# Two pairs of heads per chain step, and the output product in three groups and one, in a mixer on one core

## Chip, cores and metric

One core of one Trainium2 chip. The metric is the device time in microseconds of one execution of the whole program; of several executions the median counts.

## The reference, cut to what matters

The program computes one layer of two networks after each other on a sequence of 512 tokens of 1024 features. The change lies in the first part of the first layer, `hybrid_mixer`: a bidirectional RWKV-7 scan over 8 heads of 64, and a pooling branch, whose joined outputs are multiplied by `w_out`.

```python
def wkv7_scan(r, w, k, v, kk, a, reverse):
    def step(state, inp):
        r_t, w_t, k_t, v_t, kk_t, a_t = inp
        sa = jnp.einsum('bhvk,bhk->bhv', state, -kk_t)
        state = (state * w_t[:, :, None, :]
                 + sa[..., :, None] * (kk_t * a_t)[..., None, :]
                 + v_t[..., :, None] * k_t[..., None, :])
        return state, jnp.einsum('bhvk,bhk->bhv', state, r_t)

def hybrid_mixer(h, ...):
    ...
    for d in range(N_DIR):
        ...
        o = o + wkv7_scan(rh, heads(decay), kd, vh, kk, heads(a), reverse=(d == 1))
    ...
    return jnp.concatenate([y_rwkv, y_pool], axis=-1) @ w_out

x = x + hybrid_mixer(rmsnorm(x, norm1_w[l]), ...)
```

## The kernel before

The scan is computed in chunks of 64 tokens: 8 chunks, both directions d at once, and the heads in four pairs, 0 to 3, whose two heads e lie on the two halves of the 128 partitions. For a pair there are five pieces of work:

- *terms* (`wkv_terms`): elementwise products of the projections. They give AR (the receiving side) and BK (the sending side) of all chunks. For pairs 2 and 3 both go to memory (`spill`) and are loaded again by `wkv_load`.
- *scores* (`wkv_scores`): 64x64 products of BK with AR in each chunk (L672) and transposes of BK (L679). BK is kept with zeros beside each head's half, so that one product over all 128 partitions takes one head.
- *inverse* (`wkv_inverse`): a triangular inverse T of each chunk's 64x64 block. The diagonal blocks are solved on VectorE (L712 to L733), after a trip of the scores through memory that lays them out anew (X); T comes back through memory, and two levels of products on TensorE follow (L750, L755, L757), with copies between them. L760 is the last add of a level.
- *chain* (`wkv_chain`): the recurrence over the 8 chunks, one step after the other. A step multiplies the state Z with the scores (L801), copies to ysb on ScalarE (L803), multiplies with T (L816), copies to Z on VectorE (L820), multiplies with BN (L825) and adds the decayed state (L775, with sw from POOL, L811) to get the next state. L808 and L830 gather the output in the PSUM tile o, which L838 and L839 add into oT at the end. Each head of a pair has a PSUM tile pm of its own. The part of Z that holds the values comes from memory (vnat, L783).
- *wkv_out*: group norm, bonus and gate, with two products over 512 columns (L855, L860).

Pairs 0 and 1 have their scores and inverses beside the projections. After the projections a loop over j runs the chains of the pairs one after the other; the scores and inverse of pairs 2 and 3 are placed before or after the chains of pairs 0 and 1 by small lists (POST, INVP), and a scheduler orders each engine's instructions by their priorities (PRI, set by `hp_`). The result y of pairs 0 to 2 is written to memory and loaded again.

The output product has eight terms: a term is 128 rows of `w_out` with one y (terms 0 to 3 are the pairs of heads, 4 to 7 the pooling groups). It runs in split single precision, three products of 512 columns each for one block of 128 tokens (L129 to L131 in `mm3`; the helper `split`, L136 and L137, makes the two parts of an operand). Eight PSUM tiles `acc` hold all blocks and both halves of the columns; seven terms are added beside chain 3, the term of pair 3 last, and then eight adds (L510) bring in x.

At the start of the mixer POOL writes the zeros of BK, C and M (L242). The zeros' loop runs twice over w.C and w.M, which are two names for one tile each.

Of the kernel before, what the change touches and what calls it, by code (L numbers as in the profile page):

```python
# [9 lines left out]
F32 = mybir.dt.float32  # L10
F32R = mybir.dt.float32r
# [213 lines left out]
def mixer(g, I):  # L225
# [3 lines left out]
    with es:  # L229
        w = Ctx()  # L230
        kp = es.enter_context(tc.tile_pool(name="m_keep", bufs=1))
        w.p = es.enter_context(tc.tile_pool(name="w_p", bufs=2))
        w.a = es.enter_context(tc.tile_pool(name="w_a", bufs=2))
# [12 lines left out]
        w.pr = es.enter_context(tc.tile_pool(name="w_pr", bufs=1, space=PSUM))  # L246


        mid = es.enter_context(ExitStack())
        with ExitStack() as tmp, tc.tile_pool(name="m_h", bufs=1, side="right") as hp, tc.tile_pool(name="m_w", bufs=WINB, side="right") as wp, \  # L250
# [31 lines left out]
            w.i = mid.enter_context(tc.tile_pool(name="w_i", bufs=1, reuse_waits="tile"))  # L282
# [138 lines left out]
        rt = dict(side="right", reuse_waits="tile")  # L421
        tmp = es.enter_context(ExitStack())
        p2 = tmp.enter_context(tc.tile_pool(name="w_p2", bufs=1, reuse_waits="tile"))
        res = es.enter_context(ExitStack())
        w.z = res.enter_context(tc.tile_pool(name="w_z", bufs=3, **rt))
        aR = res.enter_context(tc.tile_pool(name="w_ar", bufs=2, **rt))
        w.y = res.enter_context(tc.tile_pool(name="w_y", bufs=2, **rt))
        w.g = res.enter_context(tc.tile_pool(name="w_g", bufs=1, **rt))
        w.pc = es.enter_context(tc.tile_pool(name="w_pc", bufs=1, space=PSUM, reuse_waits="tile"))
        for j in range(4):  # L430
            if j == 3:
                tmp.close()
# [12 lines left out]
                ys = {}
            if j < 2 and POST[j] == 0:
                with hp_(tc, PRI[20 + j]):
                    Ps.append(wkv_load(g, w, j + 2, w.p if j else p2, aR))
                with hp_(tc, PRI[10 + j]):
                    wkv_scores(g, w, Ps[j + 2])  # L450
            if j < 2 and INVP[j] == 0:
                if POST[j]:
                    with hp_(tc, PRI[20 + j]):
                        Ps.append(wkv_load(g, w, j + 2, w.p if j else p2, aR))
                    with hp_(tc, PRI[10 + j]):
                        wkv_scores(g, w, Ps[j + 2])
                with hp_(tc, PRI[8 + j]):
                    wkv_inverse(g, w, Ps[j + 2])
# [1399 lines left out]
```

## Time and profile before

| | |
|---|---|
| device time, median of 3 runs | 3271.31 us (3246.06 to 3279.7) |
| the profiled execution's own time | 3270.52 us |
| its span, first to last instruction | 3268.7 us |
| mean granted clock of TensorE | 0.947 |
| mixer | from 0 to 598 us |
| busy in the span: PE, DVE, ACT, POOL | 94%, 65%, 40%, 44% |

In the profile PE is TensorE's products, PEld its weight loads, DVE VectorE, ACT ScalarE, POOL GpSimd and SP the engine that issues most DMAs. Line numbers are those of the kernel before. A matrix product in single precision shows as two rows, and rows of products overlap, so their starts and not their durations tell how fast they go. The granted clock is the share of TensorE's full clock (2.4 GHz) that it was given; 0.50 is 1.2 GHz.

### The profile page before, as it was taken

The page shows a single profiled execution, that of the slowest core. Times are in us where ns is not written, and L with a number is a line of the kernel's source. Part 1 is how long each engine was busy: PE and PEld are TensorE (multiplying, and loading weights), DVE is VectorE, ACT ScalarE, POOL GpSimd, SP SyncE. Part 2 cuts the span into 40 slices and gives each one's busy share as a digit, 9 for nine tenths or more (in the row PEclk, how much of TensorE's full clock was granted, in tenths as well). Part 3 has the DMA queues.
Part 4 walks back from the last instruction along what each step waited for, and adds up shares of the span by engine and source line. Part 5 has one row for each costly group of instructions (what it writes and reads, how often), then busy time and mean ns, then how long its engine had stood idle before and what let it go on. Part 6 is the DMA issues. An engine that isn't in the chain of part 4 may idle for free.

```text
span 3268.7 us, 45544 instructions
## 1 busy us (share of the span) xinstructions
PE 3079.9 (94%) x16467; PEld 2632.9 (81%) x16467; DVE 2139.5 (65%) x3955; ACT 1298.5 (40%) x2244; POOL 1442.2 (44%) x1234
## 2 busy tenths in 40 slices
PE   7688999798889999999999999999999989999999
PEld 6467887687889999998998778778888878778887
DVE  5876434578997887888887876565664143456631
ACT  4333212333665333333333435564443255244431
POOL 4533222434766766667776555343222242222221
PEclk9788857899999999999999999999999999899999
DMA  5354313412447888888887874113232212132312
GB/s 171 92 121 130 81 37 112 143 46 91 155 178 267 311 302 317 303 311 306 313 313 279 285 242 145 57 48 104 97 98 90 90 62 70 39 106 94 101 61 100
DMA packets 282877, 512.30 MB, mean 157 GB/s; under 512 B 78054, under 2 KB 166902, under 8 KB 280860
## 3 DMA queue, kind: packets, MB, share of 16 engines
q1 hardware_dynamic: 244636, 373.05, 34.6%
q0 software_dynamic: 36864, 134.23, 11.5%
q8 instruction: 131, 2.15, 0.3%
q10 hardware_dynamic: 1152, 2.10, 0.2%
q14 instruction: 94, 0.77, 0.1%
HBM read 461.28 MB, written 49.99 MB: 156 GB/s over the span
## 4 chain that ended last, share of the span: by engine, by line
PE 68%; DVE 14%; DMA 6%; issue 5%; POOL 4%; ACT 2%; SPq 0%; POOLq 0%; DVEq 0%; ACTq 0%
PE pu L130 5%; PE pu L129 5%; PE pu L131 5%; DVE R L1093 4%; PE S L129 3%; PE S L131 3%; PE S L130 3%; PE o L129 3%; PE o L130 3%; PE o L131 3%; PE dn L129 2%; PE dn L130 2%; PE dn L131 2%; PE pj L129 2%; PE pj L130 2%
## 5 line engine op out<-in xcount | busy, mean ns | idle before, releaser
L129 PE MATMUL S<-hTh,uh 128*128 128x384 f32 x1024 | 362.2, 354 | 0.6 <-ACT gl L984 0.6
L131 PE MATMUL S<-hTh,ul 128*128 128x384 f32 x1024 | 347.2, 339 | 7.0 <-POOL ul L137 4.6
L130 PE MATMUL S<-hTl,uh 128*128 128x384 f32 x1024 | 346.8, 339 | 0.0
L1158 POOL TENSOR_TENSOR vl<-raw,vh 128x1024 fp32r<-128x1024 f32 (+1 forms) x128 | 282.0, 2203 | 94.3 <-ACT vh L1156 92.5
L130 PE MATMUL o<-vl,ah 128*128 128x512 f32 x768 | 299.5, 391 | 5.6 <-DVE vl L1160 5.0
L131 PE MATMUL o<-vh,al 128*128 128x512 f32 x768 | 298.2, 389 | 0.0
L129 PE MATMUL pu<-hTh,wuh 128*128 128x512 f32 (+2 forms) x736 | 282.7, 384 | 3.7 <-ACT wuh L136 3.7
L130 PE MATMUL pu<-hTl,wuh 128*128 128x512 f32 (+2 forms) x736 | 282.1, 383 | 0.0
L129 PE MATMUL o<-vh,ah 128*128 128x512 f32 x768 | 279.3, 393 | 2.4 <-ACT vh L1156 2.4
L131 PE MATMUL pu<-hTh,wul 128*128 128x512 f32 (+2 forms) x736 | 281.2, 383 | 0.0
L1132 DVE SCALAR_TENSOR_TENSOR out<-r,coef,out 128x1024 f32<-128x1024 f32 x127 | 215.9, 1700 | 64.5 <-DMA r<-in_v_r,code 63.9
L137 POOL TENSOR_TENSOR wul<-raw,wuh 128x1024 fp32r<-128x1024 f32 x44 | 106.5, 2420 | 336.8 <-ACT wuh L136 336.8
L1126 DVE SCALAR_TENSOR_TENSOR junk<-r,h 128x1024 bf16<-128x1024 f32 x128 | 203.7, 1592 | 68.5 <-DMA r<-in_u_r,code 67.8
L136 ACT ACTIVATE uh<-raw 128x1024 fp32r<-128x1024 f32 x136 | 144.3, 1061 | 252.6 <-PE S L130 210.0
L1123 POOL DMA_INDIRECT r<-in_u_r,code x128 | 164.8, 1287 | 114.5 <-DVE junk L1126 105.4
L1123 POOL DMA_INDIRECT r<-in_v_r,code x128 | 172.3, 1346 | 79.6 <-DVE out L1132 58.8
L129 PEld LDWEIGHTS S<-hTh,uh 128*128 128x128 f32 x1024 | 195.0, 190 | 9.8 <-issue 1.7
L131 PEld LDWEIGHTS S<-hTh,ul 128*128 128x128 f32 x1024 | 194.4, 190 | 8.7 <-POOL ul L137 5.2
L130 PEld LDWEIGHTS S<-hTl,uh 128*128 128x128 f32 x1024 | 195.0, 190 | 4.6
L137 POOL TENSOR_TENSOR wl<-raw,wh 128x384 fp32r<-128x384 f32 (+3 forms) x90 | 95.8, 1067 | 203.6 <-ACT wh L136 186.8
L130 PEld LDWEIGHTS o<-vl,ah 128*128 128x128 f32 x768 | 144.2, 188 | 36.6 <-DVE vl L1160 9.6
L136 ACT ACTIVATE ah<-a 128x384 fp32r<-128x384 f32 x128 | 67.0, 524 | 265.5 <-PE o L130 259.8
(513 smaller groups left out, 8136.2 us busy)
## 6 DMA issues: line engine op xcount, KB each, us to landing
raw<-in_u_l SPq DMA_DIRECT2D x128, 512.0 KB, 5.7
raw<-in_v_r SPq DMA_DIRECT2D x128, 512.0 KB, 5.3
raw<-in_w_up SPq DMA_DIRECT2D x88, 512.0 KB, 3.4
wscr<-st SPq DMA_DIRECT2D x12, 2048.0 KB, 6.9
W<-wscr SPq DMA_DIRECT2D x32, 768.0 KB, 7.6
raw<-in_w_dn SPq DMA_DIRECT2D x88, 256.0 KB, 2.5
wir<-in_w_in_l SPq DMA_DIRECT2D x38, 256.0 KB, 2.8
raw<-in_w_d_l SPq DMA_DIRECT2D x48, 192.0 KB, 2.4
```

Of the source, the lines that this page charges most:

```text
L129: nc.tensor.matmul(out=out, lhsT=l[0], rhs=r[0], start=start, stop=False)
L130: nc.tensor.matmul(out=out, lhsT=l[0], rhs=r[1], start=False, stop=False)
L131: nc.tensor.matmul(out=out, lhsT=l[1], rhs=r[0], start=False, stop=stop)
L136: nc.scalar.activation(out=hi, in_=src, func=AF.Copy)
L137: (eng or nc.vector).tensor_tensor(out=lo, in0=src, in1=hi.bitcast(F32), op=ALU.subtract)
L1093: (G if u == 1 and t0 % 16 == 0 else V).tensor_scalar(out=R[:, u], in0=iota, scalar1=i2s[:, t:t + 1], scalar2=gateT[:, t:t + 1], op0=ALU.i ...
L1123: G.indirect_dma_start(out=r, out_offset=None, in_=I["u_r" if n < 128 else "v_r"], in_offset=bass.IndirectOffsetOnAxis(ap=code3[:, s:s + 1 ...
L1126: V.scalar_tensor_tensor(out=junk, in0=r, scalar=1.0, in1=h3, op0=ALU.mult, op1=ALU.mult, accum_out=dots[:, s:s + 1])
L1132: V.scalar_tensor_tensor(out=out3, in0=r, scalar=coef[:, s:s + 1], in1=(g.x[:, 3] if s == 0 else out3), op0=ALU.mult, op1=ALU.add)
L1158: G.tensor_tensor(out=vl[:, 0:at_], in0=vraw[:, 0:at_], in1=vh[:, 0:at_].bitcast(F32), op=ALU.subtract)
```

## The change

BK loses its zero halves: it is kept as [128, 8, 2, 64], and the score products take 64 partitions each, with the two heads' products in turn. The scores and inverses of pairs 2 and 3 are emitted right behind the projections, ahead of all chains, without priorities and lists. `wkv_chains` takes two pairs and does each part of a step for both (pairs 0 and 1 first, then 2 and 3); a pair has one PSUM tile pm for both heads, and one copy to ysb. After the first two chains their pools are closed, and in that memory lie new tiles for Z, the output weights and xa, a copy of x that is loaded by one DMA of 2 MB. The output product is summed in groups of two terms, (4, 5), (6, 7), (0, 1): each group goes through a PSUM tile of six products into xa by an add on VectorE, beside chains 2 and 3. The last group (2, 3) goes into x after them. y isn't written to memory any more. `wkv_out` gets its PSUM from another pool, and its tile t shares memory with vt.

```diff
-        w.BK = [kp.tile([128, 8, 2, 2, 64], F32, name=f"BK{d}") for d in range(2)]
+        w.BK = [kp.tile([128, 8, 2, 64], F32, name=f"BK{d}") for d in range(2)]
+        w.oT = [kp.tile([128, S], F32, name=f"oT{j}") for j in range(4)]
         w.C = [kp.tile([128, 8, 128], F32, name="C")] * 2
         w.M = [kp.tile([128, 8, 128], F32, name="M")] * 2
-        for d in range(2):
-            for t in (w.BK[d].rearrange("p c e a t -> p c (e a t)"), w.C[d], w.M[d]):
-                n = t.shape[2] // 2
-                for e in range(2):
-                    G.memset(t[64 * e:64 * e + 64, :, n * (1 - e):n * (2 - e)], 0.0)
+        for t in (w.C[0], w.M[0]):
+            for e in range(2):
+                G.memset(t[64 * e:64 * e + 64, :, 64 * (1 - e):64 * (2 - e)], 0.0)
...
-        for j in range(4):
-            if j == 3:
-                tmp.close()
-                mid.close()
-                op = es.enter_context(tc.tile_pool(name="m_o", bufs=3, reuse_waits="tile"))
-                acc = {}
...
-            if j < 2 and INVP[j] == 0:
-                if POST[j]:
-                    with hp_(tc, PRI[20 + j]):
-                        Ps.append(wkv_load(g, w, j + 2, w.p if j else p2, aR))
-                    with hp_(tc, PRI[10 + j]):
-                        wkv_scores(g, w, Ps[j + 2])
-                with hp_(tc, PRI[8 + j]):
-                    wkv_inverse(g, w, Ps[j + 2])
-            with hp_(tc, PRI[j]):
-                wkv_chain(g, w, Ps[j])
...
+        pB = res.enter_context(tc.tile_pool(name="w_pb", bufs=2, side="right", **rt))
+        w.pc = es.enter_context(tc.tile_pool(name="w_pc", bufs=1, space=PSUM, **rt))
+
+        def chain_pools(st):
+            w.z = st.enter_context(tc.tile_pool(name="w_z", bufs=2, **rt))
+            w.y = st.enter_context(tc.tile_pool(name="w_y", bufs=2, **rt))
+
+        chain_pools(early)
+        for j in (2, 3):
+            Ps.append(wkv_load(g, w, j, pB, pB))
+            wkv_scores(g, w, Ps[j])
+            wkv_inverse(g, w, Ps[j])
+        wkv_chains(g, w, Ps[0:2])
+        early.close()
+        chain_pools(es)
+        op = es.enter_context(tc.tile_pool(name="m_o", bufs=3, **rt))
+        w.g = es.enter_context(tc.tile_pool(name="w_g", bufs=1, **rt))
+        xa = es.enter_context(tc.tile_pool(name="w_x", bufs=1, **rt)).tile([128, NT, D], F32, name="xa")
+        nc.sync.dma_start(out=xa, in_=I["x"].rearrange("(c p) d -> p c d", p=128))
...
+            def part(half, tb):
+                t, hs = slice(tb * 128, (tb + 1) * 128), slice(half * 512, (half + 1) * 512)
+                p = w.pi.tile([128, S], F32, tag="i", name="acc")
+                for n in range(len(ks)):
+                    mm3(nc, p, (ys[n][0][:, t], ys[n][1][:, t]), wos[half, n], n == 0, n == len(ks) - 1)
+                V.tensor_tensor(out=dst[:, tb, hs], in0=p, in1=xa[:, tb, hs], op=ALU.add)
...
+        wkv_chains(g, w, Ps[2:4])
+        ys = [wkv_out(g, w, Ps[j]) for j in range(2)]
+        out_terms((4, 5), None, xa)
+        out_terms((6, 7), None, xa)
+        out_terms((0, 1), ys, xa)
...
+        ys = [wkv_out(g, w, Ps[j]) for j in (2, 3)]
...
+        out_terms((2, 3), ys, g.x, True)
...
-            for e in range(2):
-                p = w.ps.tile([128, 4, 128], F32, tag="p", name="p")
-                for u in range(4):
-                    nc.tensor.matmul(out=p[:, u], lhsT=w.BK[d][:, c + u, e].rearrange("p a t -> p (a t)"),
-                                     rhs=P.AR[d][:, c + u], start=True, stop=True)
+            ps = [w.ps.tile([128, 4, 128], F32, tag="p", name="p") for e in range(2)]
+            for u in range(4):
+                for e, p in enumerate(ps):
+                    q = slice(64 * e, 64 * e + 64)
+                    nc.tensor.matmul(out=p[:, u], lhsT=w.BK[d][q, c + u].rearrange("p a t -> p (a t)"),
+                                     rhs=P.AR[d][q, c + u], start=True, stop=True)
...
+            P.z = P.Z[:, i % 2]
+            P.pm = w.pc.tile([128, 3, 2, 64], F32, tag=f"y{s}", name="pm")
+            for e, q in both:
+                for d in D2:
+                    nc.tensor.matmul(out=P.pm[q, 0, d], lhsT=P.sc[:, d, i, e, 0:64], rhs=P.z[:, e, d], start=True, stop=True)
+            P.y = w.y.tile([128, 2, 64], F32, tag=f"y{s}", name="ysb")
+            A.activation(out=P.y, in_=P.pm[:, 0], func=AF.Copy)
...
+        for P in Ps:
+            for e, q in both:
+                for d in D2:
+                    nc.tensor.matmul(out=P.pm[q, 1, d], lhsT=P.TT[q, d, i], rhs=P.y[q, d], start=True, stop=True)
+            for e, q in both:
+                V.tensor_copy(out=P.z[q, e], in_=P.pm[q, 1])
+        for P in Ps:
+            if i < 7:
+                for e, q in both:
+                    for d in D2:
+                        nc.tensor.matmul(out=P.pm[q, 2, d], lhsT=P.BN[:, d, i, q], rhs=P.z[:, e, d], start=True, stop=True)
+                if i % 2 == 0:
+                    for e, q in both:
+                        carry(P, P.Z[q, 1, e], e, i)
...
-    r = tp.tile([128, S], F32, tag="r", name="r")
-    t = tp.tile([128, S], F32, tag="t", name="t")
+    r = tp.tile([128, S], F32, tag="r", name="r", bufs=2)
+    t = tp.tile([128, S], F32, tag="vt", name="t")
```

What follows the mixer has the same instructions in the same order. In the mixer the orders differ; three places. The first is PE beside the inverse of pair 2, before: L750 is its first product (`T_2494`), the other rows are steps of chain 0.

```order
L830 MATMUL o<-sc,Z 64x64 x2
L808 MATMUL o<-AR,Z 64x64
L801 MATMUL pm<-Z,sc 64x64 x2
L808 MATMUL o<-AR,Z 64x64 x2
L801 MATMUL pm<-Z,sc 64x64 x2
L808 MATMUL o<-AR,Z 64x64
L750 MATMUL p<-T_2494,C 128x64 x8
L816 MATMUL pm<-ysb,TT 64x64 x4
L755 MATMUL p<-M,TT 64x64
L830 MATMUL o<-sc,Z 64x64 x2
```

After: L721 is the same product (`T_2479`), L642 and L650 are scores of pair 3, L782 and L789 the products of a step with T and BN, for two pairs.

```order
L768 MATMUL pm<-Z,sc 64x64 x4
L774 MATMUL o<-AR,Z 64x64 x3
L782 MATMUL pm<-ysb,TT 64x64 x2
L650 MATMUL p<-ident,BK_80 128x64 x8
L782 MATMUL pm<-ysb,TT 64x64 x2
L642 MATMUL p<-AR,BK_81 128x128 x3
L721 MATMUL p<-T_2479,C 128x64 x8
L642 MATMUL p<-AR,BK_81 128x128 x5
L782 MATMUL pm<-ysb,TT 64x64 x4
L789 MATMUL pm<-Z,BN 64x64 x4
```

The inverse's first product stands between a step's product with T and its product with BN now, and the scores of pair 3 stand around it instead of behind it.

The second place is SP at the end of the second chain, before: the loads of Z (L783), of y (L482) and of the output weights (L1301).

```order
L852 DMA gt<-yg 128x512
L848 DMA vt<-vts 128x512
L783 DMA Z<-vnat 64x2x64 x12
L482 DMA yl<-yg 128x512 x6
L783 DMA Z<-vnat 64x2x64 x4
L850 DMA bn<-yg 128x512
L852 DMA gt<-yg 128x512
L478 DMA yg<-r 128x512
L482 DMA yl<-yg 128x512
L1301 DMA raw<-in_w_out_l 128x512 x13
```

After: T and TT of the inverse of pair 3 (L710), xa (L439), the loads of Z for the first two steps of chains 2 and 3 (L755), the loads of `wkv_out` and the weights (L463).

```order
L707 DMA scr<-X 128x16x16
L710 DMA T_2745<-scr 64x8x64 x4
L710 DMA TT<-scr 64x8x64 x4
L439 DMA xa<-in_x 128x4x1024
L755 DMA Z<-vnat 64x2x64 x16
L815 DMA vt<-vts 128x512
L817 DMA bn<-yg 128x512
L819 DMA gt<-yg 128x512
L448 DMA yl<-yg 128x512 x2
L463 DMA wor<-in_w_out_l 128x512
```

The load of x has moved from the end of the mixer to the point between the two pairs of chains, ahead of the Z loads; the weights stand behind these.

The third place is PE at the output product, before: L129 to L131 with `acc`, among steps of chain 3.

```order
L830 MATMUL o<-sc,Z 64x64 x2
L808 MATMUL o<-AR,Z 64x64
L801 MATMUL pm<-Z,sc 64x64 x2
L808 MATMUL o<-AR,Z 64x64
L129 MATMUL acc<-wh,y_4252 128x512 x4
L808 MATMUL o<-AR,Z 64x64
L801 MATMUL pm<-Z,sc 64x64 x2
L808 MATMUL o<-AR,Z 64x64
L816 MATMUL pm<-ysb,TT 64x64 x2
L130 MATMUL acc<-wl,y_4252 128x512
L131 MATMUL acc<-wh,y_4253 128x512
L130 MATMUL acc<-wl,y_4252 128x512
```

After: the same lines, in a group of two terms (six products), among steps of chains 2 and 3 (L796, L789, L782).

```order
L796 MATMUL o<-sc,Z 64x64 x2
L789 MATMUL pm<-Z,BN 64x64 x4
L796 MATMUL o<-sc,Z 64x64 x2
L129 MATMUL acc<-wo_4127,y_4071 128x512
L130 MATMUL acc<-wo_4128,y_4071 128x512
L131 MATMUL acc<-wo_4127,y_4072 128x512
L129 MATMUL acc<-wo_4133,y_4077 128x512
L130 MATMUL acc<-wo_4134,y_4077 128x512
L131 MATMUL acc<-wo_4133,y_4078 128x512
L782 MATMUL pm<-ysb,TT 64x64 x4
L129 MATMUL acc<-wo_4127,y_4071 128x512
L130 MATMUL acc<-wo_4128,y_4071 128x512
```

A PSUM tile is complete after six products now instead of 24, and the groups stand between the halves of a step.

## Rows read from the trace of the kernel before

**Rows 1.** The page's first part: busy time, share of the span, instructions of each engine.

```profile
PE 3079.9 (94%) x16467; PEld 2632.9 (81%) x16467; DVE 2139.5 (65%) x3955; ACT 1298.5 (40%) x2244; POOL 1442.2 (44%) x1234
```

**Rows 2.** Line L510: duration min/median/max in ns, first and last start.

```profile
L510 DVE TENSOR_TENSOR x<-acc,x x8: 681/681/692, 592.6 to 597.2; 128x512 f32<-128x512 f32 x8
```

**Rows 3.** Stretches of 25 us: us, busy us (instructions) of PE PEld DVE ACT POOL, PE clock, DMA share, GB/s.

```profile
425.00:450.00 25.00, 25.00 (x141) 20.11 (x140) 6.12 (x15) 2.99 (x6) 3.32 (x4) 0.50 0.11 25
...
525.00:550.00 25.00, 23.25 (x145) 17.92 (x143) 6.94 (x17) 6.77 (x13) 5.93 (x7) 1.00 0.35 118
...
575.00:600.00 25.00, 13.87 (x44) 9.34 (x43) 14.74 (x19) 9.57 (x15) 11.97 (x9) 0.77 0.70 254
```

**Rows 4.** The same for stretches of 4 us.

```profile
342.00:346.00 4.00, 3.33 (x38) 2.52 (x36) 3.84 (x10) 0.54 (x2) 1.46 (x2) 1.00 0.08 18
346.00:350.00 4.00, 3.34 (x29) 2.85 (x27) 2.96 (x9) 0.03 (x1) 1.19 (x4) 0.54 0.34 36
...
522.00:526.00 4.00, 3.54 (x46) 3.13 (x45) 1.42 (x6) 1.08 (x4) 2.42 (x4) 0.77 0.47 159
```

**Rows 5.** Timeline of PE at half clock, chain 2: start, us, instruction, tiles.

```profile
489.24 0.69 PE L825 MATMUL pm<-Z,BN 128*64 128x64 f32 x4
...
490.78 0.47 PE L808 MATMUL o<-AR,Z 64*64 64x64 f32 x2
491.19 0.69 PE L801 MATMUL pm<-Z,sc 128*64 128x64 f32 x4
491.80 0.48 PE L808 MATMUL o<-AR,Z 64*64 64x64 f32 x4
492.21 0.69 PE L801 MATMUL pm<-Z,sc 128*64 128x64 f32 x4
...
493.99 0.69 PE L825 MATMUL pm<-Z,BN 128*64 128x64 f32 x4
```

**Rows 6.** Timeline of PE at full clock, chain 0.

```profile
310.39 0.46 PE L808 MATMUL o<-AR,Z 64*64 64x64 f32 x8
...
318.42 0.44 PE L816 MATMUL pm<-ysb,TT 64*64 64x64 f32 x4
...
329.46 0.45 PE L825 MATMUL pm<-Z,BN 128*64 128x64 f32 x4
...
332.54 0.45 PE L825 MATMUL pm<-Z,BN 128*64 128x64 f32 x4
```

**Rows 7.** Timeline of VectorE (DVE) and PE: ends of inverses and chains.

```profile
397.64 0.69 DVE L760 TENSOR_TENSOR TT<-p,TT 128x512 f32<-128x512 f32 x1 [2.12 <-PE p L757]
...
406.49 0.21 DVE L712 COPY Tb<-X 128x4 f32<-128x4 f32 x1
...
425.30 1.97 PE L750 MATMUL p<-T,C 128*128 128x64 f32 x8
...
483.02 0.69 DVE L760 TENSOR_TENSOR TT<-p,TT 128x512 f32<-128x512 f32 x1 [4.69 <-PE p L757]
...
560.29 0.41 DVE L839 TENSOR_TENSOR oT<-o,oT 128x256 f32<-128x256 f32 x1
```

**Rows 8.** Timeline of POOL at the program's start.

```profile
0.72 1.93 POOL L242 MEMSET BK<- 64x1024 f32 x2 [0.29 <-POOLq L1851]
...
9.95 0.19 POOL L159 TENSOR_SCALAR ms<-ss 128x1 f32<-128x1 f32 x1
```

**Rows 9.** DMA issues from 309 to 600 us: KB each, median us to landing.

```profile
x<-in_x SPq DMA_DIRECT2D x4, 512.0 KB, 7.2
```

**Rows 10.** The chain of waits from 560 to 600 us: start, us, what.

```profile
562.18 0.86 PE p L855 x2
...
563.27 0.24 PE acc L130
...
573.60 4.17 DMA lv<-in_lamv
...
588.64 0.43 PE acc L131
```

More of the change, by code (lines that the diff above doesn't have):

```diff
@@ L479, in mixer @@
-        early = (4, 5, 6, 7, 0, 1, 2)
-        for k in early:
-            t = op.tile([128, S], F32, tag="raw", name="yl")
-            nc.sync.dma_start(out=t, in_=g.yg[0 if k >= 4 else 2, k % 4])
-            ys[k] = tuple(op.tile([128, S], F32R, name=f"y{k}{q}", bufs=1) for q in range(2))
-            split(nc, *ys[k], t)
-        for tb in range(NT):
-            sel = int(tb >= 2)
-            acc[0, tb] = (w.ps, w.pi)[sel].tile([128, S], F32, tag="pi"[sel], name="acc")
-        with hp_(tc, PRI[22]):
-            out_terms(0, early, True, False)
@@ L490, in mixer @@
-        for tb in range(3):
-            acc[1, tb] = w.pc.tile([128, S], F32, tag=("y0", "y1", "o")[tb], name="acc")
-        out_terms(1, early, True, False, range(3))
-        ys[3] = tuple(op.tile([128, S], F32R, name=f"y3{q}", bufs=1) for q in range(2))
-        split(nc, *ys[3], y)
-        acc[1, 3] = w.pr.tile([128, S], F32, tag="r", name="acc")
-        out_terms(1, early, True, False, (3,))
-        wo = [load_w(g, op, I["w_out_l"][384:512, half * 512:(half + 1) * 512], 512, half) for half in range(2)]
@@ new lines, in mixer, with out_terms @@
+        nc.sync.dma_start(out=xa, in_=I["x"].rearrange("(c p) d -> p c d", p=128))
+        def out_terms(ks, src, dst, tiles_first=False):
+            ys = []
+            for n, k in enumerate(ks):
+                t = src[n] if src else None
+                if t is None:
+                    t = op.tile([128, S], F32, tag="raw", name="yl")
+                    nc.sync.dma_start(out=t, in_=g.yg[0, k % 4])
+                ys.append(tuple(op.tile([128, S], F32R, tag=f"y{k % 2}{q}", name=f"y{k % 2}{q}", bufs=2) for q in range(2)))
+                split(nc, *ys[-1], t)
+            wos = {}
+            def part(half, tb):
[4 more added lines that the diff above has]
+                V.tensor_tensor(out=dst[:, tb, hs], in0=p, in1=xa[:, tb, hs], op=ALU.add)
+            for half in range(2):
+                for n, k in enumerate(ks):
+                    raw = op.tile([128, S], F32, tag="raw", name="wor")
+                    nc.sync.dma_start(out=raw, in_=I["w_out_l"][k * 128:(k + 1) * 128, half * 512:(half + 1) * 512])
+                    wos[half, n] = tuple(op.tile([128, S], F32R, tag=f"wo{q}", name=f"wo{q}", bufs=4) for q in range(2))
+                    split(nc, *wos[half, n], raw, G if n % 2 else None)
+                if not tiles_first:
+                    for tb in range(NT):
+                        part(half, tb)
+            if tiles_first:
+                for tb in range(NT):
+                    for half in range(2):
+                        part(half, tb)
@@ L648, in wkv_terms @@
             nc.sync.dma_start(out=spill[d, 0], in_=AR.rearrange("p c t -> p (c t)"))
-            for e in range(2):
-                q = slice(64 * e, 64 * e + 64)
-                nc.sync.dma_start(out=spill[d, 1, q].rearrange("p (c a t) -> p c a t", c=8, a=2), in_=BK[q, :, e])
+            nc.sync.dma_start(out=spill[d, 1], in_=BK.rearrange("p c a t -> p (c a t)"))
     s = tp.tile([128, 2, S], F32, tag="u", name="s")[:, 0]
@@ L853, in wkv_out @@
     G.tensor_tensor(out=bn, in0=bn, in1=vt, op=ALU.mult)
[L854 removed]
+    p = ps.tile([128, S], F32, tag="p", name="p")
     nc.tensor.matmul(out=p, lhsT=w.bo, rhs=o, start=True, stop=True)
```

188 lines of the change are left out of this document (57 added, 131 removed).

## The prediction, made before the changed kernel was run

> **What bounds the kernel now.** I read the page's first part, then the stretches of 25 us with their granted clock, the timeline of TensorE (PE) and VectorE (DVE) for single chain steps, and last the chain of waits at the stage's end. The page shows PE busy for 94% of the span [rows 1]. The change touches only the mixer, whose last add starts at 597.2 of 3269 us [rows 2]: the order of the instructions behind the mixer is the same in both programs, so what the mixer loses or wins is what the program does, unless the clock of what follows moves.
>
> Inside the mixer the projections end ahead of 310 us, where the first chain step stands [rows 6], and stay apart from the sum but for their start. What follows, up to 598 us, is the question. There PE counts as fully busy at a granted clock of 0.50, 1.2 GHz, from 425 to 450 us, fully enough at 1.00 from 525 to 550, and for only 13.87 of 25 us from 575 to 600 [rows 3]. The clock fell at 346, after a stretch in which PE was busy for 3.33 of 4 us (VectorE solved the blocks of the inverse), and rose to 0.77 and then 1.00 about 522, ahead of the output product [rows 4].
>
> A step of the chain is bound by PE at half clock: the products with BN start at 489.24 and again at 493.99, 4.75 us apart, and the rows between leave hardly a gap [rows 5]. At full clock the same products are 3.08 us apart (329.46 and 332.54) [rows 6], less than twice as fast, so there the chain's ScalarE and VectorE work shows. The milestones are [rows 7]: the inverse of pair 2 ends with the row at 397.64 + 0.69, that of pair 3 with the one at 483.02 + 0.69, the last chain at 560.29 + 0.41. Then 37 us are left in which nothing but the last pair's output is due.
>
> **Start: -3 us.** Four memsets of BK go, two pairs of 1.93 us, and half of those of C and M, since the loop wrote each tile twice. They stand ahead of the norm's first row on POOL, at 9.95 us [rows 8]. The last token block may come late anyway, so I take 3; bounds 0 and -4 (the two pairs are 3.86).
>
> **Chains in lockstep, the core of the sum.** What two pairs side by side save is read from how rows of PE overlap. A product is two rows. At half clock four rows of L801, two products into one half of the columns, take 491.19 to 491.80, so 0.31 us a product; but the 16 rows of L825 and L830, eight products that change halves after every two, take from 489.24 to 490.78, 1.54 us or five times 0.31 [rows 5]. So where neighbours lie in different halves they overlap, and eight products in the order two, two, two, two cost five slots. In the change L768 has eight such products for two pairs (five slots, 1.5 us), L789 and L796 sixteen (nine slots, 2.8 us), L774 and L782, at about 0.20 us a product (491.80 to 492.21), five slots each (1.0 us each). That is 6.3, and I take 6.4 us for a pair step at half clock against 2 x 4.75 = 9.5 one after the other. At full clock PE would need 3.2 us, the two pairs' chain of ScalarE, VectorE and POOL more than one pair's 3.08: about 4.1 against 6.2. Bounds: 6.3 (perfect overlap) and 9.5 (none).
>
> The Trainium skill speaks against this at one place. [Rows 6] show L808 putting four products of both halves into one bank in 0.46 us, while L816 needs 0.44 for two products of one half: they overlap within a bank. "TensorEngine Tiling (Array Packing)", Gotcha 1: PSUM Pressure, says that different row tiles cannot use the same PSUM bank at the same time, and after the change the two halves of pm share one. The trace does not agree for L808. By the rule four products of a pair would cost 0.4 us more; eight steps of four pairs make 13 us of it, and the sum below would end at 3258 (rival e).
>
> **Phase 1, the two first chains beside both inverses.** In before's clock: first pair step at 315, as now (the spill's loads land no earlier). SP's order puts eight loads of Z ahead of the inverse's own stores and its load of X, so X of pair 2 lands later than now; but there is less else for PE, whose order makes chain step 3 wait for the first L721 of that inverse. I take inverse 2 done at 398 as now; 8 us later or 5 earlier are the bounds. Now VectorE begins to solve inverse 3 at 406.49, and the first product with its T starts at 425.30, 19 us later [rows 7]. After the change VectorE can begin at about 393, as T0 is free with the second level's first product: 412. Inverse 3 now takes 425.3 to 483.7, 58 us, in which 5.5 steps of chain 2 at 4.75 us (26) run too: 32 us of its own at half clock. With the last three pair steps, 19 us of which 4 lie in its waits, phase 1 ends at 412 + 47 = 459.
>
> **Between the phases: +5 us.** One load of x (2 MB) and 16 loads of Z wait for the old pools to close. Now x comes as four loads of 512 KB, each 7.2 us from issue to landing [rows 9]; after the change a load of Z, the fourth of a tile, waits for the load of x to land. I take 5 of these 7, as the first steps' other loads overlap it; bounds 4 and 9.
>
> **Phase 2, chains 2 and 3 beside the output product: 75 us.** Steps 0 to 2 at half clock, 3 x 6.4 = 19, with the four 512-column products of two wkv_out between them, 0.86 us each at full clock [rows 10], so about 2 at half, 8: 27. From step 3 on, groups of six 512-column products stand between half steps: 144 of them at 0.23 us each [rows 10] are 33 us, and five steps at full clock need 3.2 of PE each, 16: 49 us, less 1 for what overlaps. VectorE has 24 adds of 0.68 us [rows 2] more, 16 us, and was busy 6.94 of 25 us [rows 3]: hidden. So the chains end at 459 + 5 + 75 = 539 instead of 560.7: -22.
>
> **Tail: 37 us as now.** Now it is wkv_out of pair 3, a wait of 4.17 us for lv, and matmuls that go at 0.43 us [rows 10]. After the change it is two wkv_out on one VectorE and 48 products (11 us at 0.23, 21 at 0.43), less the weight splits, which can be early. Bounds 30 and 47; I take 37.
>
> Sum: -3 - 22 = -25 us, from 3270.5 us for the profiled execution (span 3268.7 and 1.8 around it), 0.8 below the median of 3271.3: 3245.
>
> **Rivals.** A measurement of this kernel can tell 1%, 33 us, from no change. (a) *The clock stays full in phase 1.* It fell after PE had idled beside VectorE's solving [rows 4]; two chains in lockstep give it more to do. For: PE would be busier in just those stretches. Against: PE's fixed order still puts step 3 behind L721. Then inverse 3 with its steps costs 28 instead of 47, and phase 2's first three steps 13 less: 3245 - 19 - 5 = 3221 if only part of the latter is won. (b) *The gain is taken back by waits.* The fixed order at L721, the Z loads behind x and the output weights behind Z on SP each add 4 to 8 us, 20 in all: 3265. For: each of these loads waits for a chain step, and SP runs in order. Against: the three lie in different places, and only what exceeds PE's own work there counts. (c) *Slower: phase 2 stays at half clock.* Before, the clock rose in a stretch of chain steps ahead of the product, and in the tail it was not held: 13.87 of 25 us busy, clock 0.77 [rows 3]. If it doesn't rise, 144 products cost 0.43 instead of 0.23, +29, five steps 3.2 more each, +16, and 48 products at the end +10, with VectorE's two wkv_out uncovered, +5: 3305. It decides from 58 us on, so all of it must come. For: groups of six products between 64-column ones are less even than before's. Against: in 525 to 550 the same mix ran at 1.00. (d) *Not what it says:* no overlap between pairs, 9.5 us a pair step. Then 3.1 us come back in each step that PE at half clock bounds, three in either phase: 3245 + 19 = 3264, as (b). (e) *Halves in one bank don't overlap*, the skill's rule above: 3258.
>
> **How the numbers follow.** Forecast 0.38, (a) 0.27, (b) with (d) 0.18, (c) 0.14, (e) 0.03. The forecast's own range is 3230 to 3258; about 0.12 of it lies under 3239 (1% below 3271). Faster by over 1%: 0.27 + 0.12 = 0.39. Slower by over 1%, above 3304: the upper part of (c) and mishaps of (b), 0.14. Within: 0.47. The range that leaves 0.2 out reaches into (a) and short of all of (c): 3205 to 3292.
>
> **What would show it.** Right: the last add into oT of chains 2 and 3 starts near 536 (539 less the 3 of the start); L796 and L789 of two pairs take near 2.8 us at half clock; inverse 3 ends near 450. Wrong: pair steps of over 8 us; a clock of 0.50 beside the 512-column products, which would give (c); PE idle for over 10 us between the phases or before the first L721; a tail of over 47 us.

## The result, and the profile after

The changed kernel takes 3228.16 us (median of 20 executions), the kernel before 3270.90 beside it: a ratio of 0.9878 (95% interval 0.9859 to 0.9898), 1.2% faster. The forecast was 3245 with a range from 3205 to 3292. In the profiled executions the span goes from 3268.7 to 3228.4 us, and all of it comes out of the mixer: its last add into x ends at 555.7 instead of 597.9 us, 42 us sooner, of which 2 are lost again behind it.

First the stretches of the changed kernel (us, busy us and instructions of PE, PEld, DVE, ACT, POOL, PE clock, DMA share, GB/s):

```profile
350.00:375.00 25.00, 24.45 (x183) 22.87 (x184) 6.97 (x17) 4.29 (x8) 6.64 (x8) 0.50 0.26 49
...
425.00:450.00 25.00, 22.09 (x259) 17.25 (x258) 10.83 (x33) 7.46 (x14) 6.06 (x13) 0.93 0.38 117
...
475.00:500.00 25.00, 25.00 (x217) 18.97 (x216) 20.81 (x45) 6.20 (x13) 10.24 (x13) 1.00 0.36 110
...
525.00:550.00 25.00, 12.32 (x29) 7.78 (x30) 13.31 (x24) 7.43 (x10) 6.00 (x3) 0.59 0.31 97
```

They answer to [rows 3]. From 425 to 450 us the granted clock is 0.93 where it was 0.50, and from 475 to 500 it is 1.00 where it was 0.50 too. In stretches of 5 us, where it fell and rose now:

```profile
330.00:335.00 5.00, 3.17 (x40) 2.72 (x39) 0.92 (x5) 0.11 (x1) 0.00 (x0) 1.00 0.73 137
335.00:340.00 5.00, 3.49 (x26) 2.96 (x26) 4.74 (x17) 0.28 (x1) 0.79 (x2) 0.67 0.04 13
...
395.00:400.00 5.00, 3.35 (x37) 3.10 (x37) 4.77 (x9) 0.00 (x0) 0.00 (x0) 0.69 0.00 0
400.00:405.00 5.00, 4.00 (x48) 3.25 (x48) 2.83 (x12) 0.56 (x2) 1.59 (x4) 0.65 0.64 84
...
410.00:415.00 5.00, 5.00 (x70) 4.65 (x70) 2.27 (x9) 1.19 (x2) 4.12 (x6) 0.50 0.01 3
415.00:420.00 5.00, 5.00 (x66) 4.73 (x67) 1.04 (x2) 1.01 (x3) 0.70 (x1) 0.98 0.00 0
```

and the kernel before, first in two stretches behind its fall at 346 us, then in the 75 us in which it stayed low:

```profile
363.00:380.00 17.00, 15.16 (x175) 13.22 (x172) 9.82 (x19) 5.79 (x8) 2.62 (x3) 0.99 0.15 25
...
391.00:414.00 23.00, 20.84 (x238) 17.79 (x238) 13.29 (x43) 5.09 (x14) 6.18 (x12) 1.00 0.19 30
...
450.00:475.00 25.00, 25.00 (x170) 22.54 (x170) 9.07 (x20) 6.67 (x13) 8.92 (x9) 0.50 0.15 48
475.00:500.00 25.00, 24.59 (x199) 21.58 (x199) 6.92 (x26) 3.97 (x13) 3.52 (x10) 0.50 0.05 12
500.00:525.00 25.00, 23.96 (x191) 18.16 (x190) 16.85 (x42) 8.57 (x21) 5.18 (x9) 0.52 0.34 106
```

So the clock is low from 336 to 415 us now, but for a short rise between 395 and 405. Before, it fell at 346, was full again from 363 to 380 and from 391 to 414, then stayed low and rose in the stretch from 522 [rows 4]. PE sent 170 to 199 rows in 25 us in that long low stretch, and sends 70 in the last 5 us ahead of the rise now; in the 5 us in which the short rise began it sent only 37, so the number of rows alone doesn't tell when the clock rises.

The timeline of VectorE gives the milestones of [rows 7]: the end of the inverse of pair 3 (L731), of chains 0 and 1 (first L806), the first copy of chain 2 (L784), two carries of a pair step (L745), the end of chains 2 and 3, the mixer's last add, and the norm behind it:

```profile
434.50 0.69 DVE L731 TENSOR_TENSOR TT<-p,TT 128x512 f32<-128x512 f32 x1 [4.45 <-PE p L728]
...
437.38 0.41 DVE L806 TENSOR_TENSOR oT<-o,oT 128x256 f32<-128x256 f32 x1
...
446.12 0.61 DVE L784 COPY Z<-pm 64x128 f32<-64x128 f32 x2 [0.46 <-PE pm L782]
...
448.08 2.02 DVE L745 SCALAR_TENSOR_TENSOR Z<-pm,WC,sw 64x64 f32<-64x64 f32 x8
...
452.61 1.49 DVE L745 SCALAR_TENSOR_TENSOR Z<-pm,WC,sw 64x64 f32<-64x64 f32 x6
...
521.86 0.41 DVE L806 TENSOR_TENSOR oT<-o,oT 128x256 f32<-128x256 f32 x1
...
555.05 0.69 DVE L458 TENSOR_TENSOR x<-acc,xa 128x512 f32<-128x512 f32 x1 [0.67 <-PE acc L131]
559.82 1.28 DVE L162 SCALAR_TENSOR_TENSOR xn<-x,rstd,wbc 128x1024 f32<-128x1024 f32 x1 [4.09 <-DMA wbc<-in_nw]
```

The inverse of pair 3 is done at 435.2 instead of 483.7, chains 0 and 1 at 437.8, and chains 2 and 3 at 522.3 where the last chain ended at 560.7. A step of two pairs takes 448.08 to 452.61, 4.53 us, at full clock. The last row shows where time is lost: the norm of the next stage waits 4.09 us for its weights. Before, the same row came 0.35 us behind the last add, so 3.7 us are lost here, of which 2 are left at the program's end.

PE, and the chain of waits at the three places where I had looked for a price:

```profile
21.23 0.58 PE L129 MATMUL pmm<-hTh,wih 128*128 128x256 f32 x1 [1.07 <-ACT wih L136]
...
410.52 1.12 PE L789 MATMUL pm<-Z,BN 128*64 128x64 f32 x16
411.37 1.12 PE L796 MATMUL o<-sc,Z 128*64 128x64 f32 x14
...
441.03 0.83 PE L768 MATMUL pm<-Z,sc 128*64 128x64 f32 x8 [2.06 <-DMA Z<-vnat]
...
446.83 0.46 PE L782 MATMUL pm<-ysb,TT 64*64 64x64 f32 x8
```

```profile
436.24 4.75 DMA Z<-vnat
...
529.41 2.57 DMA bn<-yg
...
537.20 4.56 DMA lv<-in_lamv
```

The first projection product comes at 21.23 us (before: 20.84), and waits for ScalarE's split of the weights. L782 sends eight rows, four products of both halves into one bank of pm, in 0.46 us; L816 took 0.44 for two [rows 6]. The row of Z is the wait between the phases; bn and lv are waits of the tail.

### The profile page after: what moved, and what is told of

The parts are those of the page before. It is cut to its first block, busy times and chain, and to the rows that moved or that the text cites. A ratio compares the mean times of both kernels' runs of the same rounds, so it can differ in the third digit from the quotient of the medians.

```text
span 3228.4 us, 45332 instructions
## 1 busy us (share of the span) xinstructions
PE 3028.3 (94%) x16463; PEld 2583.8 (80%) x16467; DVE 2149.9 (67%) x3974; ACT 1287.1 (40%) x2205; POOL 1439.7 (45%) x1224
## 4 chain that ended last, share of the span: by engine, by line
PE 57%; DVE 12%; DMA 10%; issue 6%; POOL 5%; ACT 1%; SPq 0%; POOLq 0%; DVEq 0%; ACTq 0%
PE pu L130 5%; PE pu L129 5%; PE pu L131 5%; DMA r<-in_v_r,code 4%; DVE R L1060 4%; DMA r<-in_u_r,code 3%; PE dn L129 2%; PE dn L131 2%; PE dn L130 2%; DVE L L1059 2%; POOL r L1090 2%; PE pj L130 2%; PE pj L129 2%; PE pj L131 2%; POOL vl L1125 2%
## 5 line engine op out<-in xcount | busy, mean ns | idle before, releaser
L129 PE MATMUL S<-hTh,uh 128*128 128x384 f32 x1024 | 361.7, 353 | 0.4 <-ACT gl L951 0.4
L131 PE MATMUL S<-hTh,ul 128*128 128x384 f32 x1024 | 346.8, 339 | 6.4 <-POOL ul L137 4.7
L131 PE MATMUL o<-vh,al 128*128 128x512 f32 x768 | 299.4, 391 | 0.0
L129 PE MATMUL pu<-hTh,wuh 128*128 128x512 f32 (+2 forms) x736 | 282.7, 384 | 3.8 <-ACT wuh L136 3.8
L129 PE MATMUL o<-vh,ah 128*128 128x512 f32 x768 | 278.8, 392 | 3.6 <-ACT vh L1123 3.6
L131 PE MATMUL pu<-hTh,wul 128*128 128x512 f32 (+2 forms) x736 | 281.2, 382 | 0.0
L1099 DVE SCALAR_TENSOR_TENSOR out<-r,coef,out 128x1024 f32<-128x1024 f32 x127 | 223.0, 1756 | 56.5 <-DMA r<-in_v_r,code 55.5
L1090 POOL DMA_INDIRECT r<-in_v_r,code x128 | 179.0, 1398 | 89.4 <-DVE out L1099 72.5
L129 PEld LDWEIGHTS S<-hTh,uh 128*128 128x128 f32 x1024 | 194.7, 190 | 9.6 <-issue 1.7
L131 PEld LDWEIGHTS S<-hTh,ul 128*128 128x128 f32 x1024 | 194.0, 189 | 9.0 <-POOL ul L137 5.3
L1123 ACT ACTIVATE vh<-raw 128x1024 fp32r<-128x1024 f32 x128 | 134.7, 1052 | 105.2 <-DMA raw<-in_v_r 101.4
```

The lines of the kernel that those rows point to most:

```text
L129: nc.tensor.matmul(out=out, lhsT=l[0], rhs=r[0], start=start, stop=False)
L131: nc.tensor.matmul(out=out, lhsT=l[1], rhs=r[0], start=False, stop=stop)
L1090: G.indirect_dma_start(out=r, out_offset=None, in_=I["u_r" if n < 128 else "v_r"], in_offset=bass.IndirectOffsetOnAxis(ap=code3[:, s:s + 1 ...
L1099: V.scalar_tensor_tensor(out=out3, in0=r, scalar=coef[:, s:s + 1], in1=(g.x[:, 3] if s == 0 else out3), op0=ALU.mult, op1=ALU.add)
L1123: A.activation(out=vh, in_=vraw, func=AF.Copy)
```

## The experiments

My theory after the result: the gain is lockstep, with a clock that is low for a shorter time; the rival: it is the new order. Each expectation has its own A and B. Each run stands beside the kernel before on its chip (medians there 3255.7 to 3258.0), so ratios are compared.

**The changed kernel once more (c)**, as the measure for the rest.

> The changed kernel itself, word for word, beside the others on one chip: 0.985 to 0.991 of the kernel before, as measured already (0.9878).

3225.78 us, 0.9897 (0.985 to 0.9944). From the first Z copy of chain 0 (311.7 us) the mixer took 238.8 us, with chains 0 and 1 done at 431.1 and chains 2 and 3 at 515.6. In the first profile it took 242.8: two executions of one kernel differ by 4 us there, and here the clock was already 0.71 from 405 to 410 us.

**One pair after the other in both phases (e1).**

```diff
-        wkv_chains(g, w, Ps[0:2])
+        wkv_chains(g, w, Ps[0:1])
+        wkv_chains(g, w, Ps[1:2])
...
-        wkv_chains(g, w, Ps[2:4])
+        wkv_chains(g, w, Ps[2:3])
+        wkv_chains(g, w, Ps[3:4])
```

> The changed kernel, but its chains take one pair after the other (0, 1, then 2, 3); all else stays. Theory A: the gain of 42 us in the mixer is mostly that two pairs' products overlap on PE and keep it at work. A pair step of two pairs takes 4.5 us at full clock (VectorE's L745 at 448.08 and 452.61) against 2 x 3.1 one after the other, so 8 pair steps per phase lose 1.7 us each at full clock and 3 at half: 15 to 25 us in each phase less what lies in the inverses' waits. It expects 3250 to 3280 us. Theory B: the gain comes from the new order (both inverses ahead of the chains, the output product in groups), and lockstep is only a form of it: within 8 us of the changed kernel, 3220 to 3236.

3282.83 us, 1.007 (1.0044 to 1.0096): the whole gain is gone, and more; even A's upper bound of 3280 is passed. Its stretches and its timelines of VectorE and PE, chain 3:

```profile
525.00:550.00 25.00, 21.39 (x164) 14.19 (x166) 12.40 (x31) 3.72 (x8) 4.49 (x7) 0.57 0.14 43
550.00:575.00 25.00, 20.48 (x178) 15.46 (x178) 7.67 (x29) 1.77 (x6) 2.38 (x6) 0.50 0.03 6
```

```profile
562.45 0.99 DVE L747 SCALAR_TENSOR_TENSOR Z<-pm,WC,sw 64x64 f32<-64x64 f32 x4 [0.94 <-PE pm L791]
...
567.30 0.99 DVE L747 SCALAR_TENSOR_TENSOR Z<-pm,WC,sw 64x64 f32<-64x64 f32 x4 [0.95 <-PE pm L791]
...
572.24 0.41 DVE L808 TENSOR_TENSOR oT<-o,oT 128x256 f32<-128x256 f32 x1
```

```profile
564.90 0.70 PE L784 MATMUL pm<-ysb,TT 64*64 64x64 f32 x8
566.09 0.69 PE L798 MATMUL o<-sc,Z 128*64 128x64 f32 x4 [0.49 <-DVE Z L786]
```

The last add of chain 3 ends at 572.7 instead of 522.3. PE runs at half clock with gaps (busy for 20.48 of 25 us), and a step of one pair takes 562.45 to 567.30, 4.85 us, about as long as in the kernel before (4.75), whose rows left hardly a gap [rows 5]. Here PE waits in each step: from L784 to L798 it is 1.19 us, with a wait of 0.49 for Z, while in e6 below PE has the other pair's row to do 0.48 us behind the same products (L782 there). The new order without lockstep (mixer's end at 602.0) is worth nothing beside the old one (597.9). The rival falls as the whole cause; no run has lockstep in the old order, so whether it needs the new one stays open.

**One pair after the other in one phase alone (e1a, e1b).** The edit is the first half of the diff above, then the second.

> The changed kernel with pairs 0 and 1 one after the other, pairs 2 and 3 in lockstep. With both phases serial the mixer ended 46 us later; of these, chains 0 and 1 ended 16 us later and chains 2 and 3 took 35 us more. Theory A (lockstep pays where chains stand alone on PE's path, that is in phase 2): here 10 to 18 us over the changed kernel, 3238 to 3246. Theory B (what matters is the clock with which phase 1 ends, which then holds in phase 2): 25 us or more over it, with a granted clock under 0.9 in the 50 us behind phase 1.

3262.69 us, 0.9995 (0.9969 to 1.0021), more than A said. Both signs of B are there, 37 us over the changed kernel and a clock of 0.77 in the 50 us behind phase 1, but B's reason is not: chains 0 and 1 end at 461.9, 31 us later than in the changed kernel beside it, and chains 2 and 3 take 79.5 us from their first copy where they took 76. So the cost lies in the first phase itself and not in the clock it leaves behind. I had put it too low, from one execution: in e1 the same first phase ended at 453.3, with a clock of 0.81 from 400 to 450 us, and here it is 0.64.

> The changed kernel with pairs 0 and 1 in lockstep, pairs 2 and 3 one after the other. Theory A (lockstep pays in phase 2): 25 to 38 us over the changed kernel, 3253 to 3266. Theory B (the clock at the end of phase 1 decides): under 15 us over it, 3228 to 3243, with the clock at 1.00 beside chain 2 as now.

3251.32 us, 0.9985 (0.9952 to 1.0017), just under A's 3253. Chains 2 and 3 take 106 us from their first copy instead of 76; of these 30 us, 5 come back in the tail (29.9 us for 34.8), and the first phase, which the edit leaves alone, was 4 shorter in this execution. Lockstep is needed in either phase.

**The output product behind the chains (e6).**

```diff
-                p = w.pi.tile([128, S], F32, tag="i", name="acc")
+                p = w.pc.tile([128, S], F32, tag=f"o{tb % 2}", name="acc")
```

> The changed kernel, but the groups of the output product take their PSUM from the chains' tiles o, so that none runs before chains 2 and 3 have ended (no further change). Theory A (the groups fill PE's waits inside the chain steps, as my forecast for the old loop would say): 144 products of 0.23 us come behind the chains, 33 us, less little: 3250 to 3262. Theory B (at two pairs a step PE is itself the bound, 4.5 us a step with hardly a gap, so the groups fill nothing): 8 pair steps of 4.5 us and then 33 us are as long as now: within 8 us, 3222 to 3238.

3227.84 us, 0.9868 (0.9825 to 0.9910): as fast as the changed kernel, and in B's range. The stretches, carries of VectorE beside chains alone, and PE's rows there:

```profile
450.00:475.00 25.00, 21.64 (x236) 17.53 (x236) 22.46 (x56) 8.34 (x19) 11.02 (x14) 0.62 0.53 163
475.00:500.00 25.00, 24.67 (x215) 19.58 (x214) 10.43 (x34) 2.02 (x6) 3.49 (x8) 0.56 0.01 3
500.00:525.00 25.00, 22.92 (x94) 17.18 (x93) 20.74 (x30) 8.54 (x15) 4.80 (x3) 1.00 0.28 93
```

```profile
477.04 0.99 DVE L745 SCALAR_TENSOR_TENSOR Z<-pm,WC,sw 64x64 f32<-64x64 f32 x4 [1.82 <-PE pm L789]
...
480.64 0.99 DVE L745 SCALAR_TENSOR_TENSOR Z<-pm,WC,sw 64x64 f32<-64x64 f32 x4 [1.82 <-PE pm L789]
...
484.25 0.99 DVE L745 SCALAR_TENSOR_TENSOR Z<-pm,WC,sw 64x64 f32<-64x64 f32 x4 [1.82 <-PE pm L789]
...
497.55 0.41 DVE L806 TENSOR_TENSOR oT<-o,oT 128x256 f32<-128x256 f32 x1
```

```profile
475.83 0.69 PE L796 MATMUL o<-sc,Z 128*64 128x64 f32 x4
476.31 0.69 PE L789 MATMUL pm<-Z,BN 128*64 128x64 f32 x8
476.79 0.63 PE L796 MATMUL o<-sc,Z 128*64 128x64 f32 x4
477.36 0.70 PE L782 MATMUL pm<-ysb,TT 64*64 64x64 f32 x8
477.84 0.63 PE L774 MATMUL o<-AR,Z 64*64 64x64 f32 x6
478.40 0.70 PE L768 MATMUL pm<-Z,sc 128*64 128x64 f32 x8
479.03 0.47 PE L774 MATMUL o<-AR,Z 64*64 64x64 f32 x2
479.43 0.69 PE L796 MATMUL o<-sc,Z 128*64 128x64 f32 x4
```

A row of carries is one pair's, and the two pairs run half a step apart: PE does one pair's products while the other pair's copies run. So a step of two pairs takes 2 x 3.61 = 7.2 us at a clock of 0.50, and PE is busy for all 10 us from 475 to 485. Against 2 x 4.85 in e1 that saves 2.5 us; at full clock lockstep saves 2 x 3.08 - 4.53 = 1.6 against the kernel before. The chains end at 498.0, 57.7 us behind their first copy (76 in the changed kernel), and the groups follow at full clock: the last add into x ends 54.6 us later (33.4). In all that is 112.3 us for 109.6, so placing the groups beside the chains is worth nothing here. But B's sum, eight steps of 4.5 us and then 33, did not run: from 455 to 491 the clock beside the chains alone was 0.54 and then 0.50. How much the groups fill when both run at full clock, this run doesn't say.

**Chains ahead of the inverses (e4).**

```diff
-        wkv_chains(g, w, Ps[0:2])
+        with hp_(tc, 600):
+            wkv_chains(g, w, Ps[0:2])
```

> The changed kernel, but the first two chains have a higher priority by 600 instructions than the scores and inverses of pairs 2 and 3, so that some 5 instead of 3.5 pair steps stand on PE ahead of the first product of the inverse. Theory A: the clock fell at 336 because PE stood behind products that wait for the second load of BK (4.17 us) and VectorE's solving; with chain steps ahead PE has work there, the clock falls later, and phase 1 ends 5 to 15 us sooner: 3213 to 3225. Theory B: the inverses are the longer line of phase 1 (X, T and T again through memory), and what delays them delays the end: 3228 to 3245.

3249.80 us, 0.9947 (0.9912 to 0.9981). Chains 0 and 1 end at 427.6, 10 us sooner than in the first profile, but the inverse of pair 3 at 467.9 instead of 435.2. This is B's reason, though the time lies above B's 3245: the inverses are the longer line of phase 1.

**Score products head by head (e2).**

```diff
-            for u in range(4):
-                for e, p in enumerate(ps):
+            for e, p in enumerate(ps):
+                for u in range(4):
```

> The changed kernel, but the score products (64 rows each) go through the four chunks of one head, then of the other, instead of in turn. Theory A (products of the two halves of the rows overlap when they are neighbours): 16 rows take 1.42 us in turn (at 317.38) and 8 rows alone 1.08, so eight such groups per pair lose 0.7 us each, 6 us a pair; of pairs 2 and 3 half is on the path: 3232 to 3240. Theory B (they don't matter for the time, the scores wait for VectorE and the loads of BK): within 3 us of the changed kernel.

3255.02 us, 0.9987 (0.9957 to 1.0017), later than either theory (the profiled execution took 3245.22). But the first Z copy already stands at 330.1 us, 18 later, and from there to the mixer's end it is 240.0 us, as in the changed kernel. The loss lies in the projections, where the stretches differ already (from 225 to 250 us PE is busy for 14.69 us at a clock of 0.51, in the changed kernel for 22.61 at 0.77); I take it that the scheduler placed other work anew, which is not shown: the slower score products of pairs 0 and 1 lie in the projections too. For pairs 2 and 3 the order of heads is worth nothing; on pairs 0 and 1 the run doesn't answer, since it changed more than I meant to change.

**The memsets back (e5).**

```diff
+        for d in range(2):
+            for e in range(2):
+                G.memset(w.BK[d][64 * e:64 * e + 64], 0.0)
+                G.memset(w.BK[d][64 * e:64 * e + 64], 0.0)
```

> The changed kernel with eight memsets of a half BK (two per half and d, some 8 us of POOL's work) back at the start, ahead of the norm's rows. My forecast (-3 us for the memsets): the first projection product, at 21.23 us now, comes 2 to 4 us later. The rival (in the changed kernel that product waits for the split of the weights on ScalarE, not for the norm): it comes at 20.5 to 22 us as before, 20.84, and as now.

One execution, 3234.94 us, so only its trace is read. The timeline of PE:

```profile
14.60 1.97 PE L171 MATMUL ptr<-ident,xn 128*128 128x128 f32 x8 [14.60 <-DVE xn L162]
...
22.52 0.58 PE L129 MATMUL pmm<-hTh,wih 128*128 128x256 f32 x1
```

The transposes wait for the norm, which stands behind POOL's memsets (14.60, in the changed kernel 8.41), but the first projection product comes 1.3 us later, at 22.52: under the forecast's 2 to 4 and above the rival's 22. In the kernel before, with 6 us more of memsets than in the changed kernel, it stood at 20.84.

**Waits taken out.** BK of pair 3 in tiles of its own (f1; its stretches of 5 us follow the numbers), then the load of x behind the first Z, two buffers in wkv_out and lv later (e8), e8 with the output behind the chains (e9), and e8 with f1 (f2).

```diff
+                w.BK = [pB.tile([128, 8, 2, 64], F32, name=f"BKx{d}", bufs=1) for d in range(2)]
...
-        nc.sync.dma_start(out=xa, in_=I["x"].rearrange("(c p) d -> p c d", p=128))
+        def load_xa(P):
+            for e in range(2):
+                q = slice(64 * e, 64 * e + 64)
+                nc.gpsimd.tensor_copy(out=xa[q, 0, 0:1], in_=P.Z[q, 0, 1 - e, 0, 0:1])
+            nc.sync.dma_start(out=xa, in_=I["x"].rearrange("(c p) d -> p c d", p=128))
...
-    vt = tp.tile([128, S], F32, tag="vt", name="vt")
+    vt = tp.tile([128, S], F32, tag="vt", name="vt", bufs=2)
```

> The changed kernel, but pair 3 loads its BK into two tiles of its own, so that its score products don't wait for those of pair 2 to be done and then for the load (BK<-spill, 4.17 us at 331.44); PE's order stays but for two places. Theory A: this wait, with VectorE's solving behind it, is what let the clock fall at 336; without it PE has work until about 342, the fall comes later or not at all, and phase 1 (first Z copy at 312.9, last oT add at 437.4, 124.5 us) is 5 to 15 us shorter. Theory B: the inverse of pair 2 with its trips through memory sets phase 1, and PE only waits elsewhere: first Z copy to last oT add stays at 118 to 126 us and the clock falls all the same.

3224.34 us, 0.9894 (0.9851 to 0.9937). From the start of the first Z copy to that of the last oT add it is 116.3 us, under B's bounds and inside A's; but runs that leave this phase as it is (c, e1b, e6, e8, e9) took 114.8 to 119.0 there, and f2 with the same edit 124.0, so this length tells nothing.

```profile
325.00:330.00 5.00, 5.00 (x67) 4.35 (x65) 2.00 (x5) 1.05 (x3) 0.00 (x0) 1.00 0.20 42
330.00:335.00 5.00, 5.00 (x43) 4.38 (x41) 0.61 (x3) 0.42 (x1) 0.00 (x0) 0.63 0.56 73
335.00:340.00 5.00, 3.25 (x25) 2.92 (x24) 4.65 (x18) 0.00 (x0) 0.80 (x2) 0.50 0.01 3
```

PE works through from 330 to 335 us, where it was busy for 3.17 of 5 us without the edit, and the clock falls all the same, even sooner. So that wait did not make it fall, and A does not hold.

> The changed kernel with three waits taken out that its trace shows: the load of x is issued behind the first Z loads of chains 2 and 3 (PE waited 2.06 us, the chain of waits 4.75 us for Z at 436.24), the tiles vt, bn and gt of wkv_out have two buffers (2.57 us for bn and 1.28 for the product with it, at 529.41), and lv is loaded behind the peer layer (4.56 us at 537.20). The theory that these waits stand on the path expects 5 to 11 us less than the changed kernel, 3217 to 3223, and at most 2 us of it lost again later. The rival (VectorE and the half clock of the tail take their place) expects within 3 us of it.

3225.96 us, 0.9895 (0.9857 to 0.9934). In its profile the waits are shorter (mixer 231.5 us from the first Z copy, 7 less), but that was the fastest of its four executions (3216.42, at a mean clock of 0.960); over the four the time is that of the changed kernel.

> e8 with the output product's groups behind chains 2 and 3 (as in e6). In e6 the clock was 0.62 and 0.56 from 450 to 500 us, beside the chains alone, and it was no slower than the changed kernel. Theory A: it fell in the wait between the phases, which e8 has shortened; then the chains run at full clock, 8 steps of 4.5 us, and the whole is 8 to 15 us under e8: 3205 to 3217. Theory B: chains alone on PE let the clock fall or leave it low wherever they stand, so it is 0.6 there again and the time is within 5 us of e8 and the changed kernel.

3228.48 us, 0.9912 (0.9880 to 0.9945). The clock was 1.00 until 450 us and then fell again beside the chains: it was 0.50 from 455 to 475, while PE was busy for 2.57 to 3.96 of each 5 us. Time and fall are B's. B's reason is not shown: from 485 the clock rose again (0.79, then 1.00) while the chains were still alone on PE.

> e8 (the load of x behind the first Z loads, two buffers in wkv_out, lv later) and f1 (pair 3's BK in tiles of its own) together, groups of the output beside the chains as in the change. In e8's profile the mixer took 231.5 us from the first Z copy to the last add into x, in the changed kernel run beside it 238.8; f1 changed nothing that could be told. Theory A (waits on the path add up): 230 us or less there, and a time 4 to 9 us under the changed kernel's 3226, 3217 to 3222, ratio to before 0.985 to 0.989. Theory B (what the waits cost is given back by the clock, which falls and rises at its own places): 3223 to 3230, ratio 0.988 to 0.992, as for the changed kernel.

3230.42 us, 0.9901 (0.9863 to 0.9938), and 244 us in its profile, where A had 230 or less. B by its ratio: none of the four versions with waits taken out can be told from the changed kernel. Each interval is 21 to 28 us wide, though, so a gain of the 5 to 11 us that e8 looked for isn't excluded either, and that the clock gives the waits back, as B has it, is not shown.

## Why the prediction was right, and where its steps were not

The direction and the range held; the gain was 43 us (42 in the mixer) where I had 25. The time, 3228.16, lies under the forecast's own 3230 to 3258 and between 3245 and rival (a)'s 3221. None of the three signs of being right came at its number (last add into oT at 521.9 for 536, L796 and L789 in 2.2 us for 2.8, inverse 3 done at 435.2 for 450), and none of the signs of being wrong came.

- **Lockstep** was the core, as forecast: without it nothing is left of the gain. How it works I had only half right. Beside the chains alone the products of the two pairs don't merge, the pairs run half a step apart, and what lockstep gives is that PE has one pair's products to do while the other pair's copies run: 3.6 us of PE's work per pair in e6, in a step that took 4.85 in e1. The step was mis-sized a little: 7.2 us at half clock for 6.4, 4.5 at full clock for 4.1. The term at fault at half clock is L774: 0.56 and 0.40 us a pair in e6's rows, so 1.9 for two pairs, where I put 1.0. [Rows 5] show it: two rows of L808, one product, take 0.41 (490.78 to 491.19), as long as four. The other terms nearly cancel (L768 1.3 for 1.5, L789 and L796 3.1 for 2.8, L782 1.0 for 1.0). Only where L789 and L796 of both pairs stand together (410.25 to 412.42, 2.2 us) were they shorter than my nine slots, 2.8.
- **One bank for both halves** (rival e): L782's rows overlap within a bank, as L808's did. The rule that the prediction takes from the Trainium skill does not show as time here.
- **Start, -3:** wrong, it gave nothing. The first transposes came at 8.41 us instead of 12.62, but the first projection product waits for the weights' split.
- **Phase 1, end at 459:** it was 437.8. This is the step that failed, by 21 us. The first product of inverse 3 stood at 406.7 instead of 412, and from there it took 31 us instead of 47: the clock rose at 415, so 23 of the 31 us ran at full clock. That is rival (a) in part, with a chance of 0.27; that it fell first, I had right. The forecast held the clock at half from its fall on. The trace of the kernel before spoke against that: it shows a full clock again from 363 to 380 and from 391 to 414 us, which I had passed over between 346 and 522.
- **Between the phases, +5:** chains 0 and 1 end at 437.8, the first product of chain 2 stands at 441.0, the first copy at 446.1, with 4.75 us for Z in the chain: as forecast, if the phases are parted at 442.8, between the two.
- **Phase 2, 75:** 522.3 - 442.8 = 79.5, though at full clock from its first steps. That it came near is luck: by the forecast's own terms, rival (a)'s 13 us less, full clock makes 62, so the rest was 17 us too low. One part is the step: 3.2 us of PE at full clock in the sum, while half of e6's 7.2 makes 3.6 by estimate and a whole step takes 4.53. Another lies from 455 to 467, where the chain of waits runs through the split of the output weights (3.30 us of it their load); the sum has nothing for it, only rival (b). From 467 on PE is the bound, busy for 52.2 of 55.3 us. How the 17 us divide is open. The price of rival (c) was not paid.
- **Tail, 37:** 33.4, and 2 us lost behind it.

From 3245 these make 3245 + 3 - 21 + 4.5 - 3.6 + 2 = 3230, the profiled execution's own time (3230.24). The sum closes because the milestones follow each other; it doesn't bear out the terms.

What was work and what was clock? On one chip, beside the second measurement, at a mean clock of 0.957 to 0.959 the kernel before took 3239.9 to 3255.7 us (five executions, median 3242.0) and the changed one 3221.9 to 3226.3 (three, median 3225.2): 17 us at equal clock. Of all 19 executions of before there, from 3277.5 us at 0.947 to 3239.9 at 0.959, a straight line makes 2.6 us for 0.001; the profiles' clocks, 0.947 and 0.956, make 23 us of that. 17 + 23 = 40 is what lies between the two profiled executions (40.3). This is an estimate from few executions, and the two parts aren't independent: work that is taken out of a stretch at half clock raises the mean clock too. What makes the clock fall and rise is open: no run here settles it, and why it rose at 415 us in the changed kernel, the largest single error of the forecast, stays open with it.

## What to carry to other kernels

Two chains whose steps alternate between small products and copies gain when they go side by side, for one chain's products fill the other's waits. Count the products from the trace's starts, line by line, and read the granted clock of the whole stretch, not only where it first falls. A wait on the chain of waits need not be worth its length: here four were removed and no change of the time could be told. Where the granted clock moves the time by more than the edit, compare executions at equal clock too.

## What I had not expected

The clock fell in a stretch where PE was busy for the full 5 us (f1, 330 to 335), and rose at 415 beside 64-column products, without a 512-column one. It also rose for a moment at 395 to 405 beside a PE that was busy for 3.35 and 4.00 of 5 us. A change of the order of two loops in the scores moved the end of the projections by 18 us; by what path, no run shows.
